# Products into one PSUM bank issued before its readers in both attentions, and the latent values' product moved between the query products and the first latent head

## The chip, the cores and the metric

The kernel runs on one core of one Trainium2 chip. A core has a matrix engine (TensorE, PE in the profile, with its weight loads as PEld), a vector engine (VectorE, DVE), a scalar engine (ScalarE, ACT), GpSimd (POOL) and a sync engine (SP) that issues most of the transfers. Each engine works through its own instruction stream in order, and semaphores hold an instruction back until what it needs is there. The metric is the device time of one execution in microseconds, as the median of several runs.

## The reference

Two encoder layers over 256 tokens of width 2048, in float32. Each layer has an attention stage with two groups of heads that share one input projection and one output projection, then a dense MLP with a squared ReLU. Every sub-layer is modulated by vectors made from a conditioning vector `c`. Cut to what matters here:

```python
for l in range(DEPTH):
    mod = silu(c) @ w_ada[l] + b_ada[l]              # 6 vectors of 2048
    h = rmsnorm(x) * (1 + sc_a) + sh_a
    dq, dk, dv, cq, ckv, kr = split(h @ w_in[l])
    # differential attention: 4 heads, each two score maps over 256 keys
    p = softmax(dq @ dk.T * scale + bias)            # m = 0, 1
    out_a = rmsnorm((p[0] - lam * p[1]) @ dv, g) * (1 - lambda_init)
    # latent attention: 8 heads, 128 plain and 64 rotary columns
    q = rmsnorm(cq, q_norm_g[l]) @ w_uq[l]
    k_nope, v_m = split(rmsnorm(ckv, kv_norm_g[l]) @ w_ukv[l])
    p = softmax((q_nope @ k_nope.T + rope(q_rope) @ rope(kr).T) * scale)
    out_b = p @ v_m
    x = x + g_a * (concat(out_a, out_b) @ w_o[l])
    h = rmsnorm(x) * (1 + sc_m) + sh_m
    x = x + g_m * (square(relu(h @ w_mlp_in[l])) @ w_mlp_out[l])
return rmsnorm(x, final_norm_g)
```

## The kernel before

**Precision and weights.** A large product is made of three: values and weights are split into a high part (rounded by a ScalarE copy, `hi`, L149) and a low part (a VectorE subtraction, `lo`, L152), and high times high, high times low and low times high are summed. Each weight block is loaded by SP into a `raw` buffer (five of them), then split in two halves by `weights` and `part`; the `hi` and `lo` buffers are four each. The modulation sums (`ada`, L378) run on VectorE; each call of `weights` issues those whose rows have come, and asks for more rows in the same five `raw` buffers.

**PSUM.** All products go to eight banks of 128 x 512 floats, each seen as two halves of 256 (`ps[:, 0]` and `ps[:, 1]`). `small` (L329) makes the products from the latent values, two column tiles to a bank `pss`; `tokens_by_k` (L287, products at L294 to L296) makes values with tokens on the partitions, in a bank `pv` for each half of the tokens.

**The attention stage in `layer`, by its names.** `col` makes a differential head's keys or queries; `probs(hd)` makes its scores and softmax with `diff_probs`; `turn(hd)` transposes the result on TensorE (`transposed`, bank `pt`, copied to `aT`). `up_r` makes the rotary queries of the latent heads, `up_k` their keys `kn`, `up_q(0)` and `up_q(1)` their plain queries `qn` in two halves, `up_v` their values `vm`. `mla` is the list of the latent heads' steps: a head's scores, then the next head's scores and this head's turn, and so on. `val` makes the differential values from `h` in eight steps, between which `interleave` places the rest of `mla` and two heads' value steps. Then follows the output projection.

In `diff_probs` a bank `psc` takes the scores of one map: for each half `t` of the queries one product into `ps[:, t]` (L1257), then VectorE adds the bias and finds the extreme in one instruction (L1258). `softmax_parts` follows with one exponential for each half on ScalarE (L1244) and a reciprocal on VectorE (L1247). In `mla_steps`, `scores` does likewise with three products for each half of the bank `psm` (L1328) and a VectorE reduction (L1329). In `diff_steps`, `values` fills both halves of `po` (L1288) with ScalarE squares as readers (L1292), and `turn` fills `pot` by transposes (L1306) with a ScalarE and a VectorE reader (L1308, L1309).

**The order.** Dependencies between instructions are found by the framework from the tiles that they touch, and a planner sets the order on each engine when the program is built; the order of the code is its starting point. `behind` adds an order by hand in some places, none of them in the lines of this change. The sequence in `layer` that the change touches is

```python
        up_q(0)
        turn(0)()
        turn(1)()
        mla[0]()
        up_v()
        turn(2)()
        for f in mla[1:3]:
            f()
        up_q(1)
```

Of the kernel before, what the change touches and what calls it, by code (L numbers as in the profile page):

```python
# [99 lines left out]
class Trunk:  # L100
# [764 lines left out]
    def layer(self, l, acc=None):  # L865
# [53 lines left out]
        def up_q(b):  # L919
            qn.extend(self.copy(ps, "qn", ms) for ps in self.small(io["w_uq"][l, b], cq, 4))  # L920
# [4 lines left out]
        def up_v():  # L925
            w = self.weights(io["w_uv"][l])
            for cg in range(2):
                pss = [self.bank("pv") for _ in range(2)]
                self.tokens_by_k(pss, [[z[:, 512 * cg : 512 * cg + 512] for z in y] for y in w], ckv, True, True)
                vm.append([self.copy(ps, "vm") for ps in pss])  # L930
# [15 lines left out]
        def turn(hd):  # L946
            return lambda: at.append(self.transposed(a[hd]))
# [33 lines left out]
                nc.sync.dma_start(self.xr[:, t], io["x"][t])  # L981
        up_q(0)
        turn(0)()
        turn(1)()
        mla[0]()
        up_v()
        turn(2)()
        for f in mla[1:3]:
            f()
# [260 lines left out]
    def diff_probs(self, l, hd, q, k):  # L1250
        nc = self.nc
        ps_, rs = [], []
        for m in range(2):
            ps = self.bank("psc")
            s, mx = self.t("s"), self.s("mx")
            for t in range(2):
                nc.tensor.matmul(ps[:, t], q[:, m, t * P : (t + 1) * P], k[:, m], start=True, stop=True)  # L1257
                nc.vector.tensor_tensor_reduce(  # L1258
                    s[:, t], ps[:, t], self.bias[:, hd, t], 1.0, 3.0e38, ALU.add, ALU.min, mx[:, t : t + 1]
                )  # L1260
            rs.append(self.softmax_parts(s, mx))
            ps_.append(s)
        c1 = self.s("c1")
        nc.vector.tensor_scalar(c1, rs[1], self.lam[:, l : l + 1], None, ALU.mult)
        a = self.u("a")
        for t in range(2):
            nc.vector.tensor_scalar(ps_[1][:, t], ps_[1][:, t], c1[:, t : t + 1], None, ALU.mult)
            nc.vector.scalar_tensor_tensor(a[:, t], ps_[0][:, t], rs[0][:, t : t + 1], ps_[1][:, t], ALU.mult, ALU.subtract)
        return a
# [8 lines left out]
    def diff_steps(self, l, hd, at, v, out):  # L1278
        nc = self.nc
        st = {}  # L1280

        def values():
            po = self.bank("po")
            junk, tot, r = self.t("osq"), self.s("otot"), self.s("or")
            for t in range(2):
                for kt in range(2):
                    c = (hd % 2) * 256
                    nc.tensor.matmul(  # L1288
                        po[:, t], at[hd][:, kt, t * P : (t + 1) * P], v[hd // 2][kt][:, c : c + 256],
                        start=kt == 0, stop=kt == 1,  # L1290
                    )
                nc.scalar.activation(junk[:, t], po[:, t], AF.Square, accum_out=tot[:, t : t + 1])  # L1292
            nc.scalar.activation(r, tot, AF.Sqrt, bias=self.eps, scale=1.0 / 256.0)
            nc.vector.reciprocal(r, r)
            o = self.t("o")
            for t in range(2):
                nc.scalar.activation(o[:, t], po[:, t], AF.Copy, scale=r[:, t : t + 1])
            st["o"] = o

        def turn():  # L1300
            o = st["o"]
            pt = self.bank("pot")
            both = [self.parts("do") for _ in range(2)]
            for d, (hi, lo, _) in enumerate(both):
                for t in range(2):
                    nc.tensor.transpose(pt[:, d, t * P : (t + 1) * P], o[:, t, d * P : (d + 1) * P], self.ident)  # L1306
                g = self.gl[:, l, d : d + 1]
                nc.scalar.activation(hi, pt[:, d], AF.Copy, scale=g)  # L1308
                nc.vector.scalar_tensor_tensor(lo, pt[:, d], g, hi.bitcast(F32), ALU.mult, ALU.subtract)  # L1309
            out.extend(both)  # L1310

        return values, turn

    def mla_steps(self, hm, qn, qr, kn, vm):
        nc = self.nc
        st = {}

        def scores():
            ps = self.bank("psm")
            s, mx = self.t("sm"), self.s("mxm")  # L1320
            for t in range(2):
                c = slice(t * P, (t + 1) * P)
                plain = (qn[hm // 2][:, hm % 2, c], kn[hm // 2][:, hm % 2])
                rope = qr[hm // 4][hm % 2][:, (hm // 2) % 2, c]
                steps = [(rope, self.kr[:, 0]), (rope, self.kr[:, 1])]
                steps.insert(2 * t, plain)
                for i, (w, x) in enumerate(steps):
                    nc.tensor.matmul(ps[:, t], w, x, start=i == 0, stop=i == 2)  # L1328
                nc.vector.tensor_scalar(s[:, t], ps[:, t], -1.0, None, ALU.mult, ALU.min, accum_out=mx[:, t : t + 1])  # L1329
            r = self.softmax_parts(s, mx)  # L1330
            for t in range(2):
                nc.scalar.activation(s[:, t], s[:, t], AF.Copy, scale=r[:, t : t + 1])
            st["s"] = s

        def turn():
            st["t"] = self.transposed(st["s"])

        def values():
            if hm % 2 == 0:
                self.pom = self.bank("pom")  # L1340
            for kt in range(2):
                c = (hm % 4) * P
                v = vm[hm // 4][kt].rearrange("p a b -> p (a b)")
                nc.tensor.matmul(self.pom[:, hm % 2], v[:, c : c + P], st["t"][:, kt], start=kt == 0, stop=kt == 1)
            if hm % 2:
                self.mo += self.split(self.pom, "mo", True)

        return scores, turn, values


# [91 lines left out]
```

## Time and profile before

| | us |
|---|---|
| median of 3 runs (2180.53 to 2183.96) | 2183.67 |
| the profiled execution | 2183.12 |
| its span in the profile | 2181.4 |
| VectorE wait on the scores' product (DVE `s` behind PE `psc`) | 3.1 |
| ScalarE wait on the score reader (ACT `s` behind DVE `mx`) | 18.5 |
| ScalarE wait on the latent score reader (ACT `sm` behind DVE `sm`) | 14.8 |

The page gives for each engine its busy time and its share of the span; a wait is idle time of an engine just before an instruction, put down to what released it. Idle time of an engine costs something only where work that ends the run stands behind it. The attention of the first layer lies at about 160 to 340 us of the span, that of the second at about 1220 to 1400 us.

### The profile page before, as it was taken

The page shows a single profiled execution, that of the slowest core. Times are in us where ns is not written, and L with a number is a line of the kernel's source. Part 1 is how long each engine was busy: PE and PEld are TensorE (multiplying, and loading weights), DVE is VectorE, ACT ScalarE, POOL GpSimd, SP SyncE. Part 2 cuts the span into 40 slices and gives each one's busy share as a digit, 9 for nine tenths or more (in the row PEclk, how much of TensorE's full clock was granted, in tenths as well). Part 3 has the DMA queues.
Part 4 walks back from the last instruction along what each step waited for, and adds up shares of the span by engine and source line. Part 5 has one row for each costly group of instructions (what it writes and reads, how often), then busy time and mean ns, then how long its engine had stood idle before and what let it go on. Part 6 is the DMA issues. An engine that isn't in the chain of part 4 may idle for free.

```text
span 2181.4 us, 29378 instructions
## 1 busy us (share of the span) xinstructions
PE 2140.9 (98%) x11494; PEld 1857.8 (85%) x11494; DVE 1599.5 (73%) x2127; ACT 1157.9 (53%) x1751; POOL 5.7 (0%) x17
## 2 busy tenths in 40 slices
PE   7998999999999999999999999999999999999998
PEld 6898888898888888888889988888888888888886
DVE  7888888888688978888876876778555555555555
ACT  6555664565455455355454575646535534644643
POOL 0000000000000000000000000000000000000000
PEclk8999999999999999999999999999999999999999
DMA  9998899799888888888967656767655554555552
GB/s 385 423 343 321 288 357 350 289 336 342 314 326 328 347 321 325 317 332 323 336 222 276 252 193 234 285 229 255 251 193 176 209 194 174 193 201 184 193 195 95
DMA packets 87244, 594.70 MB, mean 273 GB/s; under 512 B 9984, under 2 KB 10304, under 8 KB 20288
## 3 DMA queue, kind: packets, MB, share of 16 engines
q1 hardware_dynamic: 85968, 587.01, 72.8%
q0 software_dynamic: 848, 5.28, 0.6%
q8 instruction: 90, 1.47, 0.3%
q10 hardware_dynamic: 288, 0.52, 0.1%
q14 instruction: 50, 0.41, 0.0%
HBM read 589.60 MB, written 3.18 MB: 272 GB/s over the span
## 4 chain that ended last, share of the span: by engine, by line
PE 92%; DVE 4%; DMA 2%; ACT 1%; issue 0%; SPq 0%; ACTq 0%
PE ps L215 19%; PE pr L309 13%; PE pr L310 13%; PE pr L312 13%; PE ps L218 10%; PE pk L258 3%; PE pk L282 2%; PE pk L192 2%; PE pk L196 2%; PE pk L195 2%; PE pv L296 1%; PE pv L294 1%; PE pv L295 1%; DVE ada L378 1%; DVE lo L152 1%; PE pk L279 1%
## 5 line engine op out<-in xcount | busy, mean ns | idle before, releaser
L152 DVE TENSOR_TENSOR lo<-raw,hi 128x1024 fp32r<-128x1024 f32 (+1 forms) x714 | 836.4, 1195 | 440.2 <-issue 225.0
L149 ACT ACTIVATE hi<-raw 128x1024 fp32r<-128x1024 f32 (+1 forms) x714 | 733.0, 1036 | 681.6 <-PE pr L310 364.1
L378 DVE SCALAR_TENSOR_TENSOR ada<-ada,cond 128x2048 f32<-128x2048 f32 x192 | 438.4, 2286 | 11.8 <-DMA ada<-in_w_ada 11.1
L215 PE MATMUL ps<-h,hi 128*128 128x512 f32 x1856 | 431.5, 390 | 0.0
L215 PEld LDWEIGHTS ps<-h,hi 128*128 128x128 f32 x1856 | 345.1, 188 | 69.5
L309 PE MATMUL pr<-hi,hid 128*128 128x512 f32 x1024 | 398.6, 389 | 0.0
L310 PE MATMUL pr<-hi,hid 128*128 128x512 f32 x1024 | 398.4, 389 | 0.0
L312 PE MATMUL pr<-lo,hid 128*128 128x512 f32 x1024 | 253.5, 389 | 0.0
L218 PEld LDWEIGHTS ps<-h,lo 128*128 128x128 f32 x1856 | 230.3, 192 | 4.5
L218 PE MATMUL ps<-h,lo 128*128 128x256 f32 x1856 | 231.7, 283 | 0.0
L312 PEld LDWEIGHTS pr<-lo,hid 128*128 128x128 f32 x1024 | 192.3, 188 | 39.8
L309 PEld LDWEIGHTS pr<-hi,hid 128*128 128x128 f32 x1024 | 192.3, 188 | 39.7
L310 PEld LDWEIGHTS pr<-hi,hid 128*128 128x128 f32 x1024 | 192.3, 188 | 39.7
L1189 ACT ACTIVATE sum<-ps 128x256 f32<-128x256 f32 x110 | 42.1, 383 | 115.3 <-PE ps L218 114.9
L192 PE MATMUL pk<-h,hi 128*128 128x256 f32 x320 | 90.4, 285 | 0.2 <-ACT h L703 0.2
L196 PE MATMUL pk<-h,lo 128*128 128x256 f32 x320 | 90.5, 283 | 0.0
L195 PE MATMUL pk<-h,hi 128*128 128x256 f32 x320 | 90.5, 283 | 0.0
L186 DVE TENSOR_TENSOR hid<-relu,hid 128x256 fp32r<-128x256 f32 x128 | 48.4, 422 | 49.5 <-ACT hid L185 49.5
L258 PE MATMUL pk<-hf,w 128*128 128x256 f32 x384 | 84.1, 379 | 0.4 <-ACT hf L675 0.4
L258 PEld LDWEIGHTS pk<-hf,w 128*128 128x128 f32 x384 | 72.7, 190 | 10.7 <-ACT hf L675 0.8
L192 PEld LDWEIGHTS pk<-h,hi 128*128 128x128 f32 x320 | 61.2, 192 | 0.6 <-ACT h L703 0.5
L196 PEld LDWEIGHTS pk<-h,lo 128*128 128x128 f32 x320 | 61.4, 192 | 0.2 <-DVE lo L152 0.2
(239 smaller groups left out, 2482.8 us busy)
## 6 DMA issues: line engine op xcount, KB each, us to landing
raw<-in_w_m SPq DMA_DIRECT2D x238, 1024.0 KB, 5.1
ada<-in_w_ada SPq DMA_DIRECT2D x192, 1024.0 KB, 6.4
raw<-in_w_o SPq DMA_DIRECT2D x32, 1024.0 KB, 5.7
raw<-in_w_m SPq DMA_DIRECT2D x24, 768.0 KB, 5.1
raw<-in_w_dv SPq DMA_DIRECT2D x16, 1024.0 KB, 5.8
raw<-in_w_t SPq DMA_DIRECT2D x12, 1024.0 KB, 4.9
w<-in_w_a SPq DMA_DIRECT2D x24, 384.0 KB, 13.5
raw<-in_w_a SPq DMA_DIRECT2D x12, 768.0 KB, 5.4
```

The costliest lines, as they stand in the source:

```text
L149: ins = self.nc.scalar.activation(hi, v, AF.Copy)
L152: ins = self.nc.vector.tensor_tensor(lo, v, hi.bitcast(F32), ALU.subtract)
L192: ins = mm(ps, hi, x[0], start=first, stop=False, skip_group_check=shared)
L195: mm(ps, hi, x[1], start=False, stop=False, skip_group_check=shared)
L196: self.last_mac = mm(ps, lo, x[0], start=False, stop=last, skip_group_check=shared)
L215: mm(ps.rearrange("p a b -> p (a b)"), part(w, k, 0), x[2], start=k == 0, stop=False)
L218: mm(ps[:, 0], part(w, k, 1), x[0], start=False, stop=k == nk - 1)
L258: self.nc.tensor.matmul(ps, v, whole[k], start=first, stop=last, skip_group_check=True)
L309: mm(ps, xh[:, c], part(i, 0), start=kq == 0 and i == 0, stop=False)
L310: mm(ps, xl[:, c], part(i, 0), start=False, stop=False)
L312: self.last_mm = mm(ps, xh[:, c], part(i, 1), start=False, stop=kq == 3 and i == 3)
L378: ins = nc.vector.scalar_tensor_tensor(w, w, 1.0, self.cond, ALU.mult, ALU.mult, accum_out=acc[:, i : i + 1])
```

## The change

In four places the two loops over a bank's halves are parted: all products of the bank are issued first, and its readers follow. In `layer` the call of `up_v` moves up by two steps, ahead of the second differential head's turn and the first latent head's scores. Nothing else is changed; the products, the readers and the loads are the same in number, shape and result.

```diff
@@ layer
         up_q(0)
         turn(0)()
+        up_v()
         turn(1)()
         mla[0]()
-        up_v()
         turn(2)()
@@ diff_probs
             for t in range(2):
                 nc.tensor.matmul(ps[:, t], q[:, m, t * P : (t + 1) * P], k[:, m], start=True, stop=True)
+            for t in range(2):
                 nc.vector.tensor_tensor_reduce(
                     s[:, t], ps[:, t], self.bias[:, hd, t], 1.0, 3.0e38, ALU.add, ALU.min, mx[:, t : t + 1]
                 )
@@ diff_steps, values
+            for t in range(2):
                 nc.scalar.activation(junk[:, t], po[:, t], AF.Square, accum_out=tot[:, t : t + 1])
@@ diff_steps, turn
-            for d, (hi, lo, _) in enumerate(both):
+            for d in range(2):
                 for t in range(2):
                     nc.tensor.transpose(pt[:, d, t * P : (t + 1) * P], o[:, t, d * P : (d + 1) * P], self.ident)
+            for d, (hi, lo, _) in enumerate(both):
                 g = self.gl[:, l, d : d + 1]
                 nc.scalar.activation(hi, pt[:, d], AF.Copy, scale=g)
                 nc.vector.scalar_tensor_tensor(lo, pt[:, d], g, hi.bitcast(F32), ALU.mult, ALU.subtract)
@@ mla_steps, scores
                 for i, (w, x) in enumerate(steps):
                     nc.tensor.matmul(ps[:, t], w, x, start=i == 0, stop=i == 2)
+            for t in range(2):
                 nc.vector.tensor_scalar(s[:, t], ps[:, t], -1.0, None, ALU.mult, ALU.min, accum_out=mx[:, t : t + 1])
```

## The prediction

> **What bounds the kernel now.** I read the busy times first, then the chain that ended last, then TensorE's own waits (engine, tile, line and releaser: us in all, times, longest), then windows.
>
> ```profile
> span 2181.4 us, 29378 instructions
> PE 2140.9 (98%) x11494; PEld 1857.8 (85%) x11494; DVE 1599.5 (73%) x2127; ACT 1157.9 (53%) x1751; POOL 5.7 (0%) x17
> PE 92%; DVE 4%; DMA 2%; ACT 1%; issue 0%; SPq 0%; ACTq 0%
> PE psc L1257 <- DVE mx L1258: 5.4, 4, 2.9
> PE psm L1328 <- ACT qn L344: 2.6, 1, 2.6
> PE pss L192 <- ACT hi L149: 2.1, 2, 1.5
> PE psm L1328 <- DVE sm L1329: 1.7, 1, 1.7
> PE pv L295 <- DVE lo L152: 1.5, 1, 1.5
> PE pt L1275 <- ACT sm L1332: 0.6, 1, 0.6
> ```
>
> TensorE is busy 98% and carries 92% of the chain, so time is won only where it stands still or runs slowly. It is idle 2181.4 - 2140.9 = 40.5 us. The six waits shown sum to 13.9 us, all on tiles of the two attentions; the change can reach hardly any other. The first and the fourth are the form it rewrites: a product into the second half of a bank waits until VectorE has read the first half. So the program guards a bank as a whole, although the halves are disjoint.
>
> Idle time has a second price:
>
> ```profile
> 212.00:216.00 4.00, 1.22 (x2) 0.50 (x2) 2.46 (x6) 3.87 (x8) 0.00 (x0) 0.80 0.27 113
> 216.00:220.00 4.00, 2.56 (x12) 2.56 (x13) 3.92 (x7) 3.95 (x9) 0.00 (x0) 0.50 0.00 0
> 220.00:224.00 4.00, 2.89 (x16) 2.29 (x15) 2.46 (x9) 3.99 (x9) 0.00 (x0) 0.85 0.00 0
> 1280.00:1288.00 8.00, 3.56 (x21) 2.50 (x20) 7.78 (x18) 5.41 (x13) 0.00 (x0) 0.89 0.82 287
> 1288.00:1293.00 5.00, 5.00 (x13) 4.05 (x14) 0.60 (x3) 2.47 (x7) 0.00 (x0) 0.50 0.41 174
> 1296.00:1404.00 108.00, 108.00 (x538) 89.98 (x537) 72.19 (x113) 68.42 (x139) 1.05 (x2) 1.00 0.66 239
> ```
>
> Columns are the window, its length, busy time of PE, PEld, DVE, ACT and POOL (with instructions), granted clock, DMA share, GB/s. Each layer has one hole after which the clock is 0.50. In the second layer 1288 to 1293 is five busy microseconds at half clock: 2.5 us lost. The first layer's hole looks alike, but there ScalarE is full (3.87, 3.95 and 3.99 of 4): TensorE waits for an engine with no time to give. After 1296 TensorE is full at clock 1.00, with DMA at 0.66 and VectorE at 72 of 108, so what the second layer wins there should stay won.
>
> **The change, part by part.** No instruction and no DMA is added or removed, and no weight load changes its place among the loads: the turns and latent heads past which `up_v` moves load nothing. Only order and waits change. The order on an engine is made by a planner when the program is built, not by program order alone (below, the values' product stands between the two halves of one head's scores), so I forecast consequences, not an exact order.
>
> (a) Second layer: `up_v`, the latent values' product, ahead of the second differential turn and the first latent head's scores.
>
> ```profile
> 1279.37 1.22 DVE L152 TENSOR_TENSOR lo<-raw,hi 128x1024 fp32r<-128x1024 f32 x1
> 1280.91 2.29 DVE L378 SCALAR_TENSOR_TENSOR ada<-ada,cond 128x2048 f32<-128x2048 f32 x1
> 1281.59 0.49 PE L1275 MATMUL pt<-ident,a 128*128 128x128 f32 x3
> 1283.59 0.51 ACT L1244 ACTIVATE s<-s,mx 128x256 f32<-128x256 f32 x1 [0.81 <-DVE mx L1258]
> 1284.10 1.06 ACT L344 ACTIVATE qn<-pss 128x512 f32<-128x512 f32 x2
> 1284.72 0.70 PE L1328 MATMUL psm<-kn,qn 128*128 128x256 f32 x2 [2.65 <-ACT qn L344]
> 1285.50 0.40 PE L294 MATMUL pv<-hi,lath 128*128 128x512 f32 x1
> 1287.87 0.80 PE L1328 MATMUL psm<-kr,qrs 128*128 128x256 f32 x2 [1.74 <-DVE sm L1329]
> 1295.13 0.39 PE L296 MATMUL pv<-hi,latl 128*128 128x512 f32 x1
> 1295.81 0.40 PE L296 MATMUL pv<-hi,latl 128*128 128x512 f32 x1
> ```
>
> TensorE ends the transposes near 1282.08 and stands 2.65 us for the queries' copy `qn`. That copy sits on ScalarE behind an exponential, which waits for the second read of a score bank, which VectorE makes only after a 2.29 us modulation sum. TensorE then stands another 1.74 us for the reader of the first half of `psm`. Between the two the values' product begins without a wait of its own. Counting the weight loads backwards, the split that ended at 1279.37 + 1.22 = 1280.59 is its last, so all of it could run at 1282. It has 2 halves x 2 k x 2 token halves x 3 = 24 products. One round of three (1295.13 to 1295.81) takes 0.68 us at full clock, so 24 take 5.5 us: from 1282.1 to 1287.6, and by then `qn` (ended 1285.2) is there. Both holes are covered: 2.65 + 1.74 = 4.39 us. Without them the half clock has no cause: 2.5 us more. Queued behind the moved product are the second turn and the first latent head with its softmax; to hide that softmax TensorE next has the second half of `up_q`, 4 x 4 x 3 = 48 products at 0.12 us (from the rows under b), 5.8 us. If that cover fails, it costs rival C's price.
>
> (b) Second layer: differential scores in pairs.
>
> ```profile
> 1275.80 0.70 PE L1257 MATMUL psc<-k,q 128*128 128x256 f32 x2 [0.85 <-DVE mx L1258]
> 1276.57 0.28 PE L196 MATMUL pss<-lath,lo 128*128 128x256 f32 x1
> 1276.69 0.28 PE L192 MATMUL pss<-lath,hi 128*128 128x256 f32 x1
> ```
>
> The wait goes, 0.85 us, and the products behind it run at once, as they do here after it. Sum of the second layer: 4.39 + 2.5 + 0.85 = 7.7 us.
>
> (c) First layer, differential scores.
>
> ```profile
> 201.92 0.51 ACT L1244 ACTIVATE s<-s,mx 128x256 f32<-128x256 f32 x1 [0.89 <-DVE mx L1258]
> 203.52 0.51 ACT L1244 ACTIVATE s<-s,mx 128x256 f32<-128x256 f32 x1 [1.00 <-DVE mx L1258]
> 206.02 0.51 ACT L1244 ACTIVATE s<-s,mx 128x256 f32<-128x256 f32 x1 [1.90 <-DVE mx L1258]
> 206.66 0.17 DVE L1247 RECIPROCAL r<-tot 128x2 f32<-128x2 f32 x1 [0.67 <-ACT s L1244]
> 210.05 0.69 DVE L1226 TENSOR_TENSOR qrr<-qrr,sin 128x512 f32<-128x512 f32 x1 [0.92 <-ACT qrr L1224]
> 214.69 1.22 PE L1257 MATMUL psc<-k,q 128*128 128x256 f32 x2 [2.85 <-DVE mx L1258]
> 216.35 1.04 ACT L149 ACTIVATE hi<-raw 128x1024 fp32r<-128x1024 f32 x1
> 217.44 0.58 PE L192 MATMUL pss<-lath,hi 128*128 128x256 f32 x1 [1.53 <-ACT hi L149]
> ```
>
> It is tempting to book the 2.85 us. But behind that product stands the query product, which waits for weights that ScalarE splits at 216.35, inside its full stretch; issuing the scores earlier only joins two holes into one. What helps lies before it: until 206 ScalarE has room, and waits 0.89 + 1.00 + 1.90 = 3.79 us for score reads that come singly. Read in one run, the exponentials end earlier and the rotary copies queued behind them start earlier, and with them the whole full stretch. VectorE bounds this: its own waits there are 0.67 + 0.92 = 1.59 us, the rest is work that stays. Ends: -1.8 us, if three more exponentials (0.6 us each, the 0.51 and its accumulator's read) now stand before the split at 216.35; and +3.8 us, ScalarE's waits. I take 1.6, VectorE's row, as both engines must move together. The half clock of this layer stays.
>
> (d) First layer, the moved `up_v`.
>
> ```profile
> 229.88 1.22 DVE L152 TENSOR_TENSOR lo<-raw,hi 128x1024 fp32r<-128x1024 f32 x1
> 231.15 0.50 PE L295 MATMUL pv<-lo,lath 128*128 128x512 f32 x1 [1.45 <-DVE lo L152]
> ```
>
> Here its low parts come late from VectorE, whichever stands first on TensorE. The 1.45 us may grow by the half of the first head's scores that stood ahead of it (at most 0.9 us: 0.70 as in the rows of (a), and two rotary products of 0.12), or vanish if both halves stand ahead. I take 0, the middle; ends -0.9 and +1.45.
>
> (e) `psm`, `po` and `pot` elsewhere, products first. TensorE has no other wait on them in the list, so nothing is won: 0. The first reader of a bank now waits for the second product as well: at most 0.70 us for `psc`, 0.9 for `psm`. I take 0, since TensorE waits for a softmax only once, 0.6 us; the other end is rival D.
>
> [...]
>
> **Sum.** 7.7 + 1.6 + 0 = 9.3 us. The profiled execution took 2183.12 us: its span and 1.7 around it. It lies 0.55 below the median of the runs shown, 2183.67. Forecast: 2183.1 - 9.3 = **2173.8 us**.
>
> **Rivals.**
>
> A. The planner keeps the first latent head's scores ahead of the values' product. Then the second layer wins the 0.85, the exponential's 0.81 and the 1.74, 3.4 us in all; 1.8 us of hole and the half clock stay, and the first layer gives nothing: 2179.7. For it: scores stand first now. Against: the values' parts are ready 1.5 us before TensorE is free for them.
>
> B. The order changes, the time doesn't: TensorE stands as long for weights as it did for readers, as the 1.53 us at 217.44 suggests: 2183.1. Against: in the second layer the products' weights were there.
>
> C. Slower. `up_v` stood between the first latent head's scores and its transposes and hid its softmax with 5.5 us of products. If `up_q`'s second half has no weights in time, TensorE stands 5.5 us in each layer and pays 2.5 us of half clock after each: 16.0 - 7.7 = 8.3 us slower, 2191.4. It decides where that split ends later than the values' product. Against: in the second layer VectorE is so far ahead that it idles 5.15 us before its next split.
>
> ```profile
> 1295.97 1.23 DVE L152 TENSOR_TENSOR lo<-raw,hi 128x1024 fp32r<-128x1024 f32 x1 [5.15 <-ACT hi L149]
> ```
>
> D. Held-back first readers all land on the path: two layers have 16 banks of `psc` and 16 of `psm`, 16 x 0.70 + 16 x 0.9 = 25.6 us less 9.3: 2199.4. Against: the single wait of 0.6 us.
>
> [...]
>
> **Numbers.** Forecast 0.60, A 0.16, B 0.12, C 0.08, D 0.04. Range: the low end adds (c)'s other 2.2, (d)'s 1.45, the 0.6 of the last wait and the first layer's half clock (1.22 x 0.20 + 2.56 x 0.50 + 2.89 x 0.15 = 2.0), 6.3 in all: 2167; the high end is B with a microsecond: 2184. That leaves out C, D and a little below. A measurement of this kernel tells about 0.2%, 4.4 us, from no change; A lies on that edge and counts half as faster. Faster 0.68, same 0.20, slower 0.12.
>
> **What would show it.** Right: no wait of `psc` or `psm` for a reader of its own bank; in the second layer `pv` straight after the turns and clock 1.00 throughout; the first layer's drop still there, some 1.6 us earlier. Wrong: `pt` waiting for `sm` after `pv` (C); `psm` before `pv` with a wait for `qn` (A); a longer wait of `pss` for `hi` near 217 (B, or (c) below nothing).

## The result, and the profile after

| | before | after |
|---|---|---|
| median of 18 runs, us | 2183.23 (2180.37 to 2185.70) | 2179.03 (2176.80 to 2180.56) |
| the profiled execution, us | 2183.12 | 2180.51 |
| its span, us | 2181.4 | 2178.7 |

The ratio is 0.9981, interval 0.9974 to 0.9988: the change wins 4.2 us, less than half of the 9.3 forecast. The time lies inside the range, 2167 to 2184. The interval leaves out 1, so the gain is real, though small; 18 runs of each tell more than the 4.4 us that the forecast assumed. The profiled execution of after is one of its longer ones, 1.5 us above the median: what follows accounts for the 2.7 us between the two spans, not for all of the 4.2.

The page after, the lines that answer to the first ones of before:

```profile
span 2178.7 us, 29387 instructions
PE 2139.5 (98%) x11494; PEld 1862.0 (85%) x11494; DVE 1597.3 (73%) x2127; ACT 1154.7 (53%) x1751; POOL 5.7 (0%) x17
```

Idle time of TensorE is 2178.7 - 2139.5 = 39.2 us, against 40.5. So little idle time was won, although the waits that the change aims at are gone. TensorE's waits after, in the attentions and the first output projection (line and releaser: us in all, times, longest):

```profile
PE pss L192 <- ACT hi L149: 7.0, 1, 7.0
PE pt L1276 <- ACT sm L1336: 5.2, 2, 3.3
PE pr L309 <- ACT hi L149: 3.0, 3, 1.5
```

No `psc` and no `psm` waits any more. In their place stand a joined hole of 7.0 us, two waits of the first latent head's transposes `pt` for its softmax, and 3.0 us of the output projection for its weights.

To place gain and loss I take the start of the product for the norm ahead of each attention, and of the one ahead of the MLP. The rows of before, then those of after:

```profile
148.51 0.95 PE L629 MATMUL pn<-ones,acc 128*128 128x1 f32 x8
406.20 0.39 PE L1151 MATMUL pn<-ident,rms 128*128 128x128 f32 x2
1224.62 0.95 PE L629 MATMUL pn<-ones,acc 128*128 128x1 f32 x8
1464.29 0.39 PE L1151 MATMUL pn<-ident,rms 128*128 128x128 f32 x2
```

```profile
148.84 0.95 PE L629 MATMUL pn<-ones,acc 128*128 128x1 f32 x8
411.01 0.39 PE L1151 MATMUL pn<-ident,rms 128*128 128x128 f32 x2
1229.42 0.95 PE L629 MATMUL pn<-ones,acc 128*128 128x1 f32 x8
1461.63 0.39 PE L1151 MATMUL pn<-ident,rms 128*128 128x128 f32 x2
```

The second layer's attention stage goes from 239.7 to 232.2 us: **7.5 us won**, where 7.7 was forecast. The first layer's goes from 257.7 to 262.2: **4.5 us lost**, where 1.6 was to be won. What lies outside the two stages agrees within 0.4 us.

**The first layer after.** Windows of after that answer to those of before (window, its length, busy time of PE, PEld, DVE, ACT, POOL, granted clock, DMA share, GB/s):

```profile
212.00:216.00 4.00, 0.00 (x0) 0.00 (x0) 2.48 (x8) 3.56 (x8) 0.00 (x0) 0.77 0.05 20
216.00:220.00 4.00, 2.10 (x9) 1.70 (x9) 3.02 (x8) 4.00 (x8) 0.00 (x0) 0.50 0.00 0
220.00:224.00 4.00, 4.00 (x19) 4.00 (x20) 4.00 (x4) 0.67 (x1) 0.00 (x0) 0.50 0.48 139
236.00:240.00 4.00, 0.66 (x4) 0.22 (x2) 4.00 (x13) 3.46 (x8) 0.00 (x0) 1.00 0.99 340
240.00:244.00 4.00, 3.93 (x24) 3.77 (x23) 3.08 (x5) 2.55 (x8) 0.00 (x0) 0.68 0.91 338
244.00:248.00 4.00, 4.00 (x32) 4.00 (x32) 0.00 (x0) 1.38 (x2) 0.00 (x0) 0.89 0.94 342
```

Before had one drop of the clock here, after has two. The second one starts with rows that show what stands on which engine (start, length, engine, line, operation, and in brackets the idle time before and its releaser):

```profile
234.55 0.60 PE L1276 MATMUL pt<-ident,a 128*128 128x128 f32 x4
234.66 2.28 DVE L378 SCALAR_TENSOR_TENSOR ada<-ada,cond 128x2048 f32<-128x2048 f32 x1
239.28 0.90 ACT L1336 ACTIVATE sm<-sm,r 128x256 f32<-128x256 f32 x2
239.83 0.95 PE L1276 MATMUL pt<-ident,sm 128*128 128x128 f32 x4 [3.34 <-ACT sm L1336]
240.53 0.36 PE L192 MATMUL pss<-lath,hi 128*128 128x256 f32 x1
250.75 0.59 PE L294 MATMUL pv<-hi,h 128*128 128x512 f32 x1
```

The same points in before:

```profile
236.51 0.60 PE L1275 MATMUL pt<-ident,a 128*128 128x128 f32 x4
248.34 0.58 PE L294 MATMUL pv<-hi,h 128*128 128x512 f32 x1
```

At the third differential head's turn (`turn(2)`), after is 236.51 - 234.55 = 1.96 us ahead: the moved values' product runs without its wait of 1.45 us. Then TensorE has issued both heads' scores, and next in its order stand the first head's transposes, which wait for a softmax that could only begin once VectorE had done a modulation sum. The 48 products of `up_q`'s second half come behind the transposes, at 240.53. The hole is 3.34 us, and the clock drop after it is (0.32 + 0.11) x 4 x 2 = 3.4 us at half clock (0.68 and 0.89 in the last two windows), so 1.7 us more. At the first differential values' product after is 2.41 us behind: -1.96 + 3.34 + 1.7 is 3.1, less the 0.6 us that `pt` waited before.

**The second layer after.**

```profile
1280.00:1288.00 8.00, 8.00 (x54) 7.34 (x53) 7.94 (x17) 7.30 (x16) 0.00 (x0) 1.00 0.77 268
1288.00:1293.00 5.00, 5.00 (x31) 4.32 (x30) 5.00 (x11) 4.49 (x9) 0.00 (x0) 1.00 0.96 377
1293.00:1297.00 4.00, 2.12 (x14) 1.72 (x13) 1.23 (x8) 4.00 (x13) 0.00 (x0) 0.90 0.31 131
1297.00:1302.00 5.00, 5.00 (x34) 5.00 (x34) 3.06 (x2) 2.51 (x5) 0.00 (x0) 0.74 0.21 33
```

```profile
1295.37 0.33 PE L1276 MATMUL pt<-ident,sm 128*128 128x128 f32 x1 [1.88 <-ACT sm L1336]
```

From 1280 to 1293, where before had both holes, TensorE is full at clock 1.00, and the values' product follows the first turn, as forecast. Behind it the first head's softmax is uncovered here too: 1.88 us, and (0.10 x 4 + 0.26 x 5) x 2 = 3.4 us of half clock.

### The profile page after: what moved, and what is told of

It reads as the page before. It is cut to its first block, busy times and chain, and to the rows that moved or that the text cites. A ratio compares the mean times of both kernels' runs of the same rounds, so it can differ in the third digit from the quotient of the medians.

```text
span 2178.7 us, 29387 instructions
## 1 busy us (share of the span) xinstructions
PE 2139.5 (98%) x11494; PEld 1862.0 (85%) x11494; DVE 1597.3 (73%) x2127; ACT 1154.7 (53%) x1751; POOL 5.7 (0%) x17
## 4 chain that ended last, share of the span: by engine, by line
PE 88%; DVE 5%; DMA 3%; ACT 2%; issue 1%; SPq 0%; ACTq 0%; DVEq 0%
PE ps L215 19%; PE pr L309 12%; PE pr L310 12%; PE pr L312 12%; PE ps L218 10%; PE pk L258 3%; PE pk L282 2%; PE pk L192 2%; PE pk L196 2%; PE pk L195 2%; DVE ada L378 2%; DVE lo L152 2%; DMA raw<-in_w_o 1%; PE pk L279 1%; PE ps L192 1%
```

## The experiments

Each kernel was timed beside before on the same chip, and its ratio is to that. Before's median beside them was 2183.07 for `pairs_only` to `upq_mid`, 2182.53 for `q0_first` to `l1_only` and 2182.11 for the last three, so kernels of different groups are compared by ratio. In the columns of layers stand the lengths of the two attention stages, from the same two norm products, in the profiled execution, which is one run and not the median one: that of `move_only` is 2.6 us above its median, those of `psm_only` and `l1_only` 1.7 below. Two kernels with the same code in a layer show how far such a length can be trusted: `l1_only` has the first layer of before and is 2.9 us shorter there (its stage starts 1.1 us later and ends 1.7 earlier). The second layer agrees better (`after` 232.2, `move_l1` 232.3, `l1_only` 230.7).

| kernel | median us | ratio (95%) | first layer | second layer |
|---|---|---|---|---|
| before | 2183.23 | 1 | 257.7 | 239.7 |
| after | 2179.03 | 0.9981 (0.9974 to 0.9988) | 262.2 | 232.2 |
| pairs_only | 2177.11 | 0.9974 (0.9963 to 0.9984) | 257.1 | 233.2 |
| move_only | 2183.22 | 1.0001 (0.9992 to 1.0010) | 264.0 | 236.2 |
| move_l1 | 2174.82 | 0.9962 (0.9950 to 0.9975) | 258.7 | 232.3 |
| upq_mid | 2173.69 | 0.9954 (0.9941 to 0.9966) | 257.7 | 228.6 |
| q0_first | 2171.17 | 0.9944 (0.9932 to 0.9957) | 254.6 | 228.6 |
| psc_only | 2182.78 | 1.0000 (0.9991 to 1.0009) | 256.6 | 238.3 |
| psm_only | 2178.70 | 0.9982 (0.9973 to 0.9990) | 257.5 | 234.3 |
| l1_only | 2174.13 | 0.9957 (0.9945 to 0.9970) | 254.8 | 230.7 |
| before_fewer | 2181.72 | 0.9997 (0.9989 to 1.0006) | 255.0 | 239.3 |
| after_fewer | 2175.85 | 0.9975 (0.9966 to 0.9984) | 256.9 | 232.3 |
| upq_mid_fewer | 2166.90 | 0.9932 (0.9919 to 0.9944) | 251.5 | 228.6 |

### What cost the first layer its time: the move or the pairs

My theory, T1: the moved `up_v` uncovers the first latent head's softmax. The rival, T2: the paired scores themselves cost the first layer. First the change without the move (against the change):

```diff
         turn(0)()
-        up_v()
         turn(1)()
         mla[0]()
+        up_v()
         turn(2)()
```

> The four pairings without moving up_v. Theory T1 (the first layer's 4.8 us loss comes from the moved up_v, which leaves the first latent head's softmax uncovered: a 3.3 us hole before its transposes and a half-clock window after it; the pairings cost nothing): the first layer's end comes back to within 2 us of before, the second layer keeps only 2 to 4 us of its 7.4 because the queries' copy is waited for again; 2178 to 2181. Rival T2 (the paired scores themselves cost the first layer, by the joined 7.0 us hole and its three half-clock windows, and the move is neutral there): the first layer still ends some 4.8 us late, and the second wins 2 to 4: 2184 to 2186.

2177.11 us, and a first layer as long as before's: T1's direction, a microsecond better than its figures.

The move alone (against before):

```diff
         turn(0)()
+        up_v()
         turn(1)()
         mla[0]()
-        up_v()
         turn(2)()
```

> up_v moved, no pairing. T1: the first layer loses 3 to 5 us to a wait of the first latent head's transposes for its softmax, the second layer wins about 6 to 7 (the hole at the queries' copy is filled): 2179 to 2182. T2: nothing lost in the first layer, 6 to 7 won in the second: 2176 to 2177.

2183.22 us: above both, far from T2. I had let the second layer keep the move's whole gain; in the profiled execution, a long one, it won 3.5 us there and lost 6.3 in the first.

Both pairings, the move in the second layer alone (against the change):

```diff
         turn(0)()
-        up_v()
+        if l:
+            up_v()
         turn(1)()
         mla[0]()
+        if l == 0:
+            up_v()
         turn(2)()
```

> All four pairings in both layers, up_v moved in the second layer only. T1: first layer within 2 us of before, second layer wins 7.4: 2174 to 2177. T2: first layer 4.8 us late as in the change, second wins 7.4: 2180 to 2181.

2174.82 us, inside T1's figures; T2 falls. The move costs the whole kernel some 4 us through the first layer.

If the softmax is what is uncovered, an earlier second half of `up_q` should cover it. `mla[1]` is the second head's scores, `mla[2]` the first head's transposes (against the change):

```diff
         turn(2)()
-        for f in mla[1:3]:
-            f()
+        mla[1]()
         up_q(1)
+        mla[2]()
         turn(3)()
```

> The whole change, and up_q(1) called one step earlier, between the second latent head's scores and the first head's transposes, so that its 48 products (5.8 us) stand where the softmax is waited for. T1: both holes before those transposes (3.3 and 1.9 us) and the half-clock windows after them (3.4 us each at half: 1.7 us) go; 3.3 + 1.7 + 1.9 + 1.7 = 8.6 us less than the change, perhaps two less if another wait follows: 2170 to 2173. T2: the first layer stays late by what its scores cost, only the second layer's 3.6 us come back: 2175 to 2176.

2173.69 us, just above T1's figures and below T2's. The same stretch of TensorE as shown of after:

```profile
235.27 0.60 PE L1331 MATMUL psm<-kn,qn 128*128 128x256 f32 x2
235.52 0.47 PE L192 MATMUL pss<-lath,hi 128*128 128x256 f32 x1
```

The query products follow the scores at 235.52 with no wait: their weights were there, and only the place of the transposes had held them until 240.53 in after. No wait for `sm` is left in either layer. Beside its own before, 2183.07, `upq_mid` wins 9.4 us.

### Which pair won the second layer

> before with the pairing of the differential scores (psc) alone. Theory P1 (the second layer's gain of the pairings, 6.4 us by the marks of pairs_only, comes from the differential scores, whose early exponentials let the queries' copy qn run earlier): second layer 4 to 6.5 us shorter than before, 2177 to 2179. Rival P2 (it comes from the first latent head's scores, whose second half no longer waits for the first half's reader): second layer at most 2 us shorter, 2181 to 2183.5.

> before with the pairing of the latent heads' scores (psm) alone. Theory P1: second layer at most 2.5 us shorter than before (the wait of 1.74 us goes and little else), 2181 to 2183.5. Rival P2: second layer 4 to 6.5 us shorter, 2177 to 2179. If the two halves of the half-clock stretch are what counts, each alone gives part and the parts do not add up to 6.4.

Each has one edit of the diff alone, on before: in `psc_only`

```diff
@@ diff_probs
                 nc.tensor.matmul(ps[:, t], q[:, m, t * P : (t + 1) * P], k[:, m], start=True, stop=True)
+            for t in range(2):
```

and in `psm_only`

```diff
@@ mla_steps, scores
                     nc.tensor.matmul(ps[:, t], w, x, start=i == 0, stop=i == 2)
+            for t in range(2):
```

`psc_only` is 1.0000, its second layer 1.3 us shorter; `psm_only` 0.9982 and 5.4. So P1 falls and P2 holds. The window 1270 to 1300, one row each of before, `psc_only` and `psm_only`:

```profile
1270.00:1300.00 30.00, 24.71 (x145) 21.45 (x144) 21.50 (x44) 22.14 (x44) 0.00 (x0) 0.89 0.48 176
```

```profile
1270.00:1300.00 30.00, 24.47 (x150) 21.68 (x149) 22.11 (x42) 21.70 (x45) 0.00 (x0) 0.89 0.53 185
```

```profile
1270.00:1300.00 30.00, 26.44 (x182) 24.15 (x181) 23.72 (x47) 24.71 (x50) 0.00 (x0) 1.00 0.61 224
```

Clock 0.89 over 30 us is 6.6 us at half speed. With the `psm` pairing alone the clock stays at 1.00 in the profiled execution, though the larger hole is still there:

```profile
PE psm L1328 <- ACT qn L344: 2.6, 1, 2.6
```

It is tempting to say that only the two holes together, 2.65 and 1.74 us with a short run of products between them, halve the clock. `before_fewer` (below), whose second layer has the code of before, contradicts it: its larger hole (2.6 us) ends at 1283.30 and its smaller one (1.2 us) begins at 1285.24, and the clock falls between the two, with TensorE busy:

```profile
1283.30:1283.90 0.60, 0.60 (x3) 0.55 (x4) 0.60 (x2) 0.60 (x2) 0.00 (x0) 1.00 1.08 369
1283.90:1285.20 1.30, 1.30 (x5) 0.62 (x3) 1.26 (x5) 0.81 (x2) 0.00 (x0) 0.51 0.98 416
```

So the larger hole was enough there, and a hole of the same length was not in `psm_only`. What the smaller hole adds is not settled: before and `psc_only`, which have both holes, show 6.8 us at half clock, `pairs_only`, with one hole of 3.2 us, shows 3.4 (clock 0.79 over the 8 us from 1280). `psm_only` therefore shows that its pairing wins the wait of 1.74 us, and that without the second hole no half clock followed in this execution; 1.74 and the 2.5 us of half clock make 4.2 of its 5.4 us. That execution is the fastest of 11, so a usual one may win less.

### What the first layer's pairings are worth

The first layer of before, the second of the change (at each of the four pairings, and at `up_v` as in `move_l1`, the layer decides):

```diff
@@ diff_probs
             for t in range(2):
                 nc.tensor.matmul(ps[:, t], q[:, m, t * P : (t + 1) * P], k[:, m], start=True, stop=True)
-            for t in range(2):
+                if l == 0:
+                    reader(t)
+            if l:
+                for t in range(2):
+                    reader(t)
```

> The first layer as before in every respect, the second as in the change: pairings and the moved values' product. Theory T1 (the change's gain of 7.4 us is the second layer's alone and the first layer's pairings are worth nothing): 2174.5 to 2176.5, equal to move_l1 within 1 us. Rival T3 (the first layer's pairings win the 1.6 us of the prediction's term c): 1 to 2.5 us above move_l1. If they cost: below move_l1.

0.9957 beside 0.9962 of `move_l1`: the same within the measurement, so the first layer's pairings win nothing that shows, and T3, the forecast's 1.6 us, is not borne out.

### Why nothing was won before 218 us

In `q0_first` the call of `up_q(0)` stands ahead of `probs(3)` in the first layer, on top of `upq_mid`:

```diff
+        if l == 0:
+            up_q(0)
         probs(3)()
...
-        up_q(0)
+        if l:
+            up_q(0)
         turn(0)()
```

> upq_mid with the first layer's up_q first half called before the last differential head's softmax, so that ScalarE's split of its weights no longer stands behind four exponentials and the key copies. Theory H1 (the 7.0 us hole at 211 to 218 us is ScalarE's order): the wait of pss for hi falls from 7.0 to at most 2 us, two or three half-clock windows of the first layer become one or none, and the time is 5 to 8 us under upq_mid: 2166 to 2169. Rival H2 (ScalarE is full in that stretch, whatever stands first): what the split wins, the exponentials and the key copies give back as waits of the turns or of psm, and the time is that of upq_mid, 2172 to 2175.

Neither figure: 2171.17 us, between them. ScalarE's split and TensorE's waits in that stretch are now:

```profile
213.05 2.00 ACT L149 ACTIVATE hi<-raw 128x1024 fp32r<-128x1024 f32 x2
```

```profile
PE pss L192 <- ACT hi L149: 2.9, 1, 2.9
PE pv L294 <- ACT hi L149: 1.5, 1, 1.5
```

In after the split stands behind the key copies and a head's exponentials:

```profile
213.70 2.07 ACT L344 ACTIVATE kn<-pss 128x512 f32<-128x512 f32 x4
216.79 2.94 ACT L149 ACTIVATE hi<-raw 128x1024 fp32r<-128x1024 f32 x3
217.88 0.58 PE L192 MATMUL pss<-lath,hi 128*128 128x256 f32 x1 [7.02 <-ACT hi L149]
```

The hole of 7.0 us becomes 2.9 + 1.5, so ScalarE's order made part of it; what makes the rest is open. `q0_first` is the quickest kernel here with the whole computation, but against `upq_mid` the intervals overlap, so the gain of some 2 us is likely and not shown.

### Where an earlier first layer goes

`upq_mid` has no uncovered softmax left, and yet a first layer as long as before's. Two rows each of before, after and `upq_mid`, over the output projection:

```profile
340.00:372.00 32.00, 32.00 (x143) 26.48 (x142) 28.71 (x31) 12.84 (x18) 0.00 (x0) 1.00 0.89 332
372.00:404.00 32.00, 31.07 (x137) 25.23 (x136) 28.32 (x35) 13.87 (x19) 0.00 (x0) 1.00 0.95 364
```

```profile
340.00:372.00 32.00, 31.51 (x140) 25.74 (x139) 27.88 (x32) 12.18 (x19) 0.00 (x0) 1.00 0.91 331
372.00:404.00 32.00, 29.54 (x129) 23.57 (x128) 29.32 (x33) 13.39 (x16) 0.00 (x0) 1.00 0.96 349
```

```profile
340.00:372.00 32.00, 29.91 (x125) 24.26 (x124) 26.37 (x30) 11.98 (x16) 0.00 (x0) 0.95 0.87 310
372.00:404.00 32.00, 30.98 (x137) 25.35 (x136) 27.53 (x32) 13.78 (x19) 0.00 (x0) 1.00 0.95 356
```

TensorE is full in before but for 0.93 us; the two others stand some 3 us there, with the transfers at 0.87 to 0.96. The test is this edit, which leaves out six loads, on before, on the change and on `upq_mid`:

```diff
-        w = self.wp.tile([P, D], F32, tag="raw", name=self.name("ada"), bufs=5)
         l, g, i = self.ada_todo.pop(0)
-        self.nc.sync.dma_start(w, self.io["w_ada"][l, NK * g + i])
+        if l == 0 and g in (3, 4) and i in (7, 9, 11):
+            w = self.ada_last[g]
+        else:
+            w = self.wp.tile([P, D], F32, tag="raw", name=self.name("ada"), bufs=5)
+            self.nc.sync.dma_start(w, self.io["w_ada"][l, NK * g + i])
+            self.ada_last[g] = w
```

> before with six of the modulation rows' loads left out (rows 7, 9 and 11 of the first layer's fourth and fifth vectors, 1 MB each, due at about 330 to 390 us); the row before stands in for each, so VectorE makes as many sums. Theory L1 (in the first layer TensorE meets the output projection's weights as they arrive, so that what its attention wins is waited for there): before has one such wait of 0.9 us, it goes, and the time is at most 1.5 us under before: 2181.5 to 2183.5. Rival L2 (transfers set nothing there): 2182 to 2184, the same within the measurement; this run is the yardstick for the other two.

> The change with the same six loads left out. Theory L1: the three waits of pr for hi, 3.0 us, go, the first layer is 2 to 3 us shorter than the change's, and the time is 2175.5 to 2177.5. Rival L2 (the first layer's loss is the hole of 3.3 us and its half clock alone, and the weights come no earlier): 2178 to 2180, the change's.

> upq_mid with the same six loads left out. Theory L1: its waits of pr for hi, 3.1 us, and the half clock of the stretch from 340 to 372 us (0.95) go: 3 to 4 us less than upq_mid, 2169.5 to 2171. Rival L2: 2172.5 to 2174.5, that of upq_mid.

Before gives 0.9997, no difference. `upq_mid` goes to 2166.90 us, below L1's figures; by ratio, 0.9954 to 0.9932, that is some 5 us, and the two intervals just meet. The change goes to 2175.85 us, inside L1's figures, but its ratio, 0.9975, is not clear of the 0.9981 without the edit. `upq_mid_fewer` in the same windows:

```profile
340.00:372.00 32.00, 32.00 (x143) 26.50 (x142) 30.89 (x36) 14.08 (x19) 0.00 (x0) 1.00 0.80 285
372.00:404.00 32.00, 32.00 (x157) 26.81 (x156) 24.93 (x33) 14.62 (x24) 0.00 (x0) 1.00 0.73 264
```

TensorE is full at clock 1.00, the DMA share has fallen to 0.80 and 0.73, and no wait of `pr` is left, here or in `after_fewer`. That bears L1 out: part of what the first layer's attention wins is waited for at the output projection's weights. In before the same loads gone win nothing that shows (0.9989 to 1.0006); there one wait of 0.9 us stood. `upq_mid_fewer`'s first layer is 6.2 us shorter than `upq_mid`'s: 3.1 are the waits and about 1.6 the half clock (0.95 over 32 us); the rest, about 1.5, I cannot place. The edit does not tell two causes apart: the six rows take a share of the transfers, and they also hold `raw` buffers that the weights need.

## Why the prediction failed

**(a), the moved product in the second layer.** The order came as forecast, and the sum of (a) and (b) came out, 7.5 us for 7.7, but that is luck, for it is made up of other terms. Forecast were 5.2 us of idle time and 2.5 of half clock. In the second layer's stage TensorE is busy 234.34 of 239.67 us before and 230.33 of 232.21 after: its idle time falls by 3.4 us only. The half clock falls by 0.8 (2.5 to 1.7). The other 3.2 us were won within its busy time, for which the forecast had no term. The pairings win them: before, less its 2.5 of half clock, makes 231.8 us of busy time; `psm_only` has 230.65 at clock 1.00, and `pairs_only` 230.08 with about 1.5 of half clock, thus 228.6. A bank's products now stand in one run on TensorE instead of two; that this is how the time goes is not shown. Two of the forecast's terms were also booked to the wrong part. The pairing of `psm` alone wins the 1.74 us, and (e) had priced it at 0. Beside both pairings the move adds 1.0 us in the change (233.2 to 232.2), and 4.6 where the softmax is covered (233.2 to 228.6): the hole of 3.2 us left in `pairs_only` and its piece of half clock. The uncovered softmax took 3.6 of it back (232.2 against 228.6), 1.88 of hole and 1.7 of half clock.

**The step that failed** is the sentence in (a) that to hide the first latent head's softmax "TensorE next has the second half of `up_q`", and its silence in (d), where I took 0 for the first layer. Next in TensorE's order stood that head's own transposes, with the 48 products behind them. The order of the calls says so already: `mla[2]`, the transposes, stands ahead of `up_q(1)`. In place of the cover the runs show 3.34 us of hole and 1.7 of half clock in the first layer, 1.88 and 1.7 in the second. With the cover put in (`upq_mid`) the kernel wins 9.4 us where 9.3 was forecast; that figure too is luck, since in its profiled execution the second layer wins 11.0 and the first nothing. Rival C named the mechanism and the price's two parts: 5.5 us of hole and 2.5 of half clock a layer, both too large. Its deciding point was wrong, though: not a late split of the weights, since `upq_mid` finds them ready, but the order. At a chance of 0.08 it was priced too low for an event that only needed the order of five calls to be read.

**(b)** `psc` in the second layer: 0.85 forecast, 1.3 by the length of the layer, nothing that the times can tell. In `psc_only` the wait is gone, but the two holes behind it have grown from 2.65 and 1.74 to 3.15 and 2.38 us, so the idle time only moved.

**(c)** The first layer's scores in pairs: 1.6 forecast, 0 found (`l1_only` beside `move_l1`). Rows of after show where it stopped:

```profile
200.53 0.60 ACT L344 ACTIVATE qr<-pss 128x512 f32<-128x512 f32 x1 [0.97 <-PE pss L196]
206.58 1.28 ACT L1233 ACTIVATE qrs<-qr 64x512 fp32r<-64x512 f32 x2 [3.05 <-DVE qr L1228]
```

```profile
207.00 0.59 ACT L344 ACTIVATE qr<-pss 128x512 f32<-128x512 f32 x1
```

The last row is before's. The rotary copy came at 200.53 instead of 207.00, as meant, and then ScalarE waited 3.05 us for the rotary arithmetic, which VectorE made behind a modulation sum (202.32 to 204.53). The query product starts at 217.88 (shown above), 0.44 later than before. The remark that earlier scores "only join two holes into one" was right.

**(d)** The 1.45 us of `pv` went (the favourable end), and was lost again to the softmax. **(e)** is wrong for `psm`, as said; of the first readers held back (rival D) nothing shows: `pairs_only` holds them all and is faster. With one bank and its products issued first, no product of `psc` or `psm` waits for a reader in after, where before waited 5.4 and 1.7 us. Whether two banks would do the same was not tried.

**The last 2 us.** At the output projection the first layer lost 2.0 us more (TensorE busy 32.00 + 31.07 before, 31.51 + 29.54 after) in waits for weights. No term or rival had that: I looked at the DMA share for the second layer, 0.66, and not for the first, 0.95 at the output projection.

## What to carry to other kernels

When work is moved away, ask what it hid, and look up what stands next in the engine's order and what that waits for; here one call put one place earlier turned 0.9981 into 0.9954. A short hole can cost more than its length, through the half clock behind it (here 3.34 us of hole and 1.7 of half clock), and two executions with equal holes can differ in that (0.94 and 1.00 over 30 us, behind 1.88 and 1.89 us). Read the transfers' share at the place where the gain would arrive: at stretches that had 0.89 and 0.95 in before, waits of 3.0 us stood in after and 3.1 in `upq_mid`.

## What the runs showed of the hardware that was not expected

In these executions the half clock came in pieces of about 3.4 us: from the windows, 3.4 us in after at 240, 6.8 in before at 212 to 224 ((0.20 + 0.50 + 0.15) x 4 x 2), 10.2 in after from 212 to 228 ((0.23 + 0.50 + 0.50 + 0.05) x 4 x 2; the clock is 0.95 from 224 to 228). The length of a hole did not fix how many pieces followed it. After 2.6 us the clock fell to 0.51 in `before_fewer` and stayed at 1.00 in `psm_only`, as shown above. After and `l1_only` have the same code in the second layer and the same wait there, 1.88 us (shown above) and in `l1_only` 1.89:

```profile
1288.83 0.33 PE L1286 MATMUL pt<-ident,sm 128*128 128x128 f32 x1 [1.89 <-ACT sm L1363]
```

`l1_only` kept the clock at 1.00 (the window 1270 to 1300 of `l1_only`, then of after):

```profile
1270.00:1300.00 30.00, 28.11 (x189) 25.59 (x188) 25.21 (x51) 25.49 (x53) 0.00 (x0) 1.00 0.65 239
```

```profile
1270.00:1300.00 30.00, 28.12 (x188) 26.16 (x187) 24.26 (x47) 26.74 (x53) 0.00 (x0) 0.94 0.53 194
```

That is 1.5 us of difference between two programs that are equal in this layer (230.7 and 232.2). `move_l1` and `after_fewer`, with this code there too, have after's length (232.3 each). Holes of 1.88 and 2.6 us had a drop of the clock behind them in some executions and none in others. Rival A let the half clock stay behind a hole of 1.8 us: after bears that out, `l1_only` does not.
